# Smaller blocks in a triangular inverse, and another placing of the weight splits, in a two-layer hybrid trunk

## The chip, the cores and the metric

The kernel runs on one core of a Trainium2 chip. The metric is device time in microseconds (us) of one execution. The core's engines run side by side, each through a queue of its own in a fixed order: TensorE (PE, matrix products), VectorE (DVE), ScalarE (ACT), GpSimd (POOL) and SyncE (SP, here only an issuer of transfers).

## The reference

A causal decoder trunk of two layers for 256 tokens of width 1024, all in float32:

```
for each layer:
    x = LN(alpha * x + mixer(x))
    x = LN(alpha * x + relu(x @ W_in)**2 @ W_out)
layer 0 mixer: RWKV-7 time mixing (8 heads x 64) beside a block-sparse attention (4 heads x 128)
layer 1 mixer: dilated attention, three groups of 8 query heads x 128 over 8 shared k/v heads
RWKV-7, per head, for each token:
    S = S * w_t + (S @ a_t) b_t^T + v_t k_t^T ;  y_t = S @ r_t
```

The rest of the time mixing (token shift, decay, norms, gate, bonus) is done per token. With 256 tokens the sparse attention has one block and is plain causal attention.

## The kernel before, in words

**Weights.** All weights are 211 chunks of 128x1024 floats (512 KB), loaded in order by `Stream` into a ring of raw tiles (`load`, line 90, issued on SP). A chunk of number under `UNSPLIT` (17) is used as it is: a float32 product, which runs on PE in two passes. A later chunk is split (`split`): ACT casts the high part `hi` (line 95), DVE, or POOL for the twelve chunks listed in `ON_POOL`, subtracts to get the low part `lo` (line 97). A product with split operands is three passes, high by high, high by low and low by high (lines 225 and 230 to 232). The `hi`/`lo` tiles form a ring of places: `NW1` (4) in the first part, four more (`NW2`) from layer 0's MLP on. A split waits for a raw tile that has arrived and for a place that PE has left; the load of a raw tile waits for the split, or the product, that frees it.

**Order.** The Python order of the calls gives priorities; a scheduler then fixes one order for each engine when the kernel is built. `tc.high_priority()` and `early(...)` move work ahead. At run time an engine takes its queue strictly in order.

**First part (layer 0).** Chunks: 0 (`zwa`), 1 to 4 (k), 5 to 8 (v), 9 to 12 (`mv_chunk`, the attention's v), 13 to 16 (`r_proj`), 17 and 18 (`g_proj`), 19 to 26 (`m_proj`, the attention's q and k). `x_part` splits the input x into `xh` and `xl` for the three-pass products. RWKV-7 goes in two chunks of 128 tokens (c = 0, 1). For each the recurrence becomes a triangular system per head, whose unit triangular 128x128 matrix has to be inverted: `ab_mm` computes the strictly triangular part `abT[c]` and writes it to DRAM (`dA`); `g_load` (line 624) fetches the 64 diagonal blocks of 32x32 (16 matrices of four blocks), one per partition, into `gA`; `g_steps` inverts all of them on DVE by substitution, 31 steps of two instructions (lines 682, 684) of 31 to 256 elements; `g_back` writes the inverses to DRAM (`dT`, line 690) and reads them back as `Tall` (line 691) with a block's rows on partitions. `t_start` transposes them on DVE (line 746). Then PE doubles the block size: `w32`/`t32` go from 32 to 64 (line 757 multiplies `Tall` with `abT`), `w64`/`t64` from 64 to 128. `bk_step` transposes Bt and Kt (line 717), `mk_step` makes the masked products of a head (mask on DVE, line 655), `bonus` uses `bones` (line 644), and `gate_step` the gate.

The substitution step, j from 0 to 30:

```
n, m = 31 - j, j + 1
tmp[a, b] = gA[:, j, j + 1 + a] * gI[:, j, b]      # n x m, line 682
gI[:, j + 1:32, 0:m] += tmp                        # line 684
```

**Tails.** Every LayerNorm stands in a `tail`: DVE forms u and its statistics as the products of 128 tokens end (lines 260, 261), aggregates them (271, 272), POOL takes the power -0.5 of the variance (line 273), DVE scales (285, 286), PE transposes x (`trans`, line 297), ACT and DVE split it (`split_evac`, line 241). Token block 0 is normalized while PE multiplies for block 1. The MLP's first eight chunks follow (`by_token`; the squared relu is lines 414 to 416).

Of the kernel before, what the change touches and what calls it, by code (L numbers as in the profile page):

```python
# [36 lines left out]

NCHUNK = 211

UNSPLIT = 17  # L40
ON_POOL = (34, 36, 37, 38, 39, 42, 100, 150, 151, 161, 164, 169)


STATIONARY = [1] * 9 + [0] * 4 + [1] * 14 + [0] * 8
_MLP = [0] * 8 + [1] * 8 + [0] * 16 + ([1] * 8 + [0] * 8) * 2
STATIONARY += _MLP + [0] * 4 + [1] * 32 + [0] * 12 + _MLP
LINE, STAT_AT = 64, 56
NW1, NW2, NR, NR2 = 4, 4, 4, 2
NS4, NS2 = 13, 6
RIGHT = "right"  # L50
HS = 8 * (16 * P + 16)
NZ = 15
PC_MIX, PC_W0, PC_A0, PC_KK, PC_KA, PC_RK, PC_LG, PC_LB = 0, 15, 19, 23, 27, 31, 35, 39
NPAR = 43
# [72 lines left out]
def trunk(ctx: ExitStack, tc: tile.TileContext, w_all, x_nat, x_t, par_in, lora_in, gup2_in, ln_in,  # L127
# [35 lines left out]
    def tok_s(tok):  # L163
        return slice(tok * P, tok * P + P)
# [46 lines left out]
    def xraw(k):  # L211
        return xst[k // 2][:, k % 2]
# [237 lines left out]
    yl = [const.tile([P, 4, T], F32R, name=f"yl{i}") for i in range(2)]  # L450
    lora = pa.tile([P, 2, 512], F32, name="lora")
    nc.sync.dma_start(out=lora, in_=lora_in)
    bones = pa.tile([P, P], F32, name="bones")
    nc.sync.dma_start(out=bones, in_=bones_in)
    pmf = pa.tile([P, 4, P], F32, tag="s2", name="pmf", bufs=NS2)
    pmask = pa.tile([P, 4, P], U8, name="pmask")
    gup2 = pa.tile([P, 512], F32, name="gup2")
# [158 lines left out]
        dst = bass.AP(tensor=dA.tensor, offset=dA.offset + c * 8 * HS, ap=[[P, P], [HS, 8], [1, P]])  # L616
        nc.scalar.dma_start(out=dst, in_=abT[c])

    gA = pa.tile([64, 32, 32], F32, name="gA")
    gI = pa.tile([64, 32, 32], F32, name="gI")  # L620
    gtmp = pa.tile([64, 256], F32, name="gtmp")

    def g_load():
        nc.sync.dma_start(out=gA, in_=bass.AP(tensor=dA.tensor, offset=dA.offset, ap=[[32 * P + 32, 64], [P, 32], [1, 32]]))

    pend = pa.tile([P, 4, 1], F32, name="pend")

# [35 lines left out]
    def g_init():  # L663
        for c in range(2):
            nc.gpsimd.memset(X64s[c][0:32, :, 32:64], 0.0)
        nc.gpsimd.memset(gI, 0.0)
        nc.gpsimd.memset(gI.rearrange("p a b -> p (a b)")[:, 0:1024:33], 1.0)

    def ab_init(c):
        abT[c] = v8(s4(f"abT{c}"))  # L670
# [6 lines left out]

    def g_steps_(j0, j1):
        for j in range(j0, j1):
            n, m = 31 - j, j + 1  # L680
            tmp = gtmp[:, 0:n * m].rearrange("p (a b) -> p a b", a=n)
            nc.vector.tensor_tensor(tmp, gA[:, j, j + 1:32].unsqueeze(2).to_broadcast([64, n, m]),
                                    gI[:, j:j + 1, 0:m].to_broadcast([64, n, m]), MUL)
            nc.vector.tensor_tensor(gI[:, j + 1:32, 0:m], gI[:, j + 1:32, 0:m], tmp, ADD)


    Tall = pa.tile([P, 16, 32], F32, name="Tall")

    def g_back():
        nc.sync.dma_start(out=dT.rearrange("(p n) -> p n", p=64), in_=gI.rearrange("p a b -> p (a b)"))  # L690
        nc.sync.dma_start(out=Tall, in_=bass.AP(tensor=dT.tensor, offset=dT.offset, ap=[[32, P], [4096, 16], [1, 32]]))

    zg = {}
# [31 lines left out]
    def mv_chunk(ch):  # L725
        if ch == 0:
            accv.extend(bank(True) for t in range(2))
        hl = nxt()
        for kk in range(2):
            k = ch * 2 + kk  # L730
            for tok in range(2):
                nc.tensor.matmul(accv[tok], xraw(k)[:, tok_s(tok)], hl[:, half(kk)], start=k == 0, stop=k == KT - 1)

    def mv_end():
        vb = MV["vb"] = s4("vb").rearrange("p (c v) -> p c v", c=2)
# [4 lines left out]
    Tc, TTc, TT, Wc, X64 = {}, {}, {}, {}, {}  # L740
    odd = [(slice(b, b + 32), slice(b + 32, b + 64)) for b in (0, 64)]

    def t_start(c):
        Tc[c] = Tall[:, c * 8:c * 8 + 8, :]
        TTc[c] = pa.tile([P, 8, 32], F32, tag="TTc", name="TTc", bufs=2)
        nc.vector.transpose(TTc[c].rearrange("p h s -> p (h s)"), Tc[c].rearrange("p h s -> p (h s)"))
        TT[c] = v8(s4(f"TT{c}"))
        nc.gpsimd.memset(TT[c], 0.0)
        for b in range(0, P, 32):
            nc.scalar.copy(TT[c][b:b + 32, :, b:b + 32], TTc[c][b:b + 32])  # L750
# [251 lines left out]
    g_steps(12, 18)
    r_proj(0)
    r_proj(1)
    r_proj(2)
    mk_step(0, range(0, 4))
    g_steps(18, 24)
    bonus(0)
    g_steps(24, 31)
    r_proj(3)  # L1010
    g_back()
    s_init()
    t_start(0)
    g_proj(0)
# [280 lines left out]
def _constants():  # L1295
    f = np.float32
    half = 16
    inv = (f(500000.0) ** (-np.arange(half, dtype=f) / f(half))).astype(f)
    ang = np.arange(T, dtype=f)[None, :] * inv[:, None]
    cos, sin = np.cos(ang).astype(f), np.sin(ang).astype(f)  # L1300
    ropec = np.concatenate([cos, cos], axis=0)
    ropes = np.concatenate([-sin, sin], axis=0)
    ropec, ropes = [np.tile(t, (4, 1)) for t in (ropec, ropes)]
    t = np.arange(T)
    dist = t[:, None] - t[None, :]

    def add(ok):
        return np.where(ok, f(0), f(NEG)).astype(f)

    causal = add(dist >= 0)  # L1310
    cmask = np.concatenate([causal[:P, :P], causal[P:, :]], axis=1)
    gs = [add((dist >= 0) & (dist <= 128)), add((dist >= 0) & (dist % 4 == 0)), add((dist >= 0) & (dist % 16 == 0))]
    dmask = np.concatenate([g[:P, :P] for g in gs] + [g[P:, :] for g in gs], axis=1)
    s = np.arange(P)
    strict = (s[:, None] < s[None, :])
    incl = (s[:, None] <= s[None, :])
    pmask = np.stack([incl, strict, incl, strict], axis=1).astype(f)
    bones = (s[:, None] // 64 == s[None, :] // 64).astype(f)
# [22 lines left out]
```

## Time and profile before

| | |
|---|---|
| median of three runs | 721.17 us (720.55 to 723.44) |
| the profiled execution | 720.38 us |
| its span in the trace | 718.6 us |
| PE busy | 97% of the span |
| DVE, ACT, POOL busy | 65%, 48%, 10% |
| weight splits on DVE, on POOL | 182 and 12 |
| mean granted TensorE clock | 0.992 of full speed |

The profile is of one execution. Busy time counts an engine as working while an instruction runs; a row of a timeline gives start, duration, the instruction with its tiles, and in brackets the idle time of that engine ahead of it with what ended the wait.

### The profile page before, as it was taken

What the parts mean: (1) busy time and instruction counts of PE and PEld (TensorE: products, weight loads), DVE (VectorE), ACT (ScalarE), POOL (GpSimd) and SP (SyncE); (2) the same over time, 40 slices, a digit from 0 to 9 for tenths busy, and PEclk for the clock granted to TensorE, in tenths of its full rate; (3) what the DMA queues carried; (4) which work ended last, traced back from release to release, by engine and by line L of the source; (5) the groups of instructions that cost most, each with busy time, mean ns of one, the idle gap of its engine ahead of it and who ended that gap; (6) DMA issues with size and microseconds to landing.
All of it is one profiled execution on the core that took longest, in us unless ns stands there. A gap on an engine that the chain in (4) does not pass through costs nothing. (4 is left out here: it accounts for less than half of the span.)

```text
span 718.6 us, 11530 instructions
## 1 busy us (share of the span) xinstructions
PE 696.8 (97%) x4572; PEld 621.0 (86%) x4572; DVE 463.7 (65%) x753; ACT 344.4 (48%) x515; POOL 70.9 (10%) x75
## 2 busy tenths in 40 slices
PE   9999999997999999999999999999999999999995
PEld 7867898986889889989879999998878888998985
DVE  3747985659686445546597767775488654464645
ACT  4712357253375335445164666656337543454520
POOL 3000000026100000000020121111131110000002
PEclk9999999998999999999999999999999999999998
DMA  8366362156584666565078543444357465655401
GB/s 322 123 185 192 132 189 77 60 179 237 171 292 148 205 201 192 192 193 191 29 263 304 165 152 126 166 151 157 106 160 258 162 201 186 204 182 187 133 1 59
DMA packets 40759, 122.74 MB, mean 171 GB/s; under 512 B 8129, under 2 KB 11073, under 8 KB 40577
## 3 DMA queue, kind: packets, MB, share of 16 engines
q1 hardware_dynamic: 38048, 120.07, 50.9%
q10 hardware_dynamic: 2656, 1.93, 0.9%
q8 instruction: 36, 0.59, 0.3%
q14 instruction: 19, 0.15, 0.1%
HBM read 119.63 MB, written 2.36 MB: 170 GB/s over the span
## 5 line engine op out<-in xcount | busy, mean ns | idle before, releaser
L97 DVE TENSOR_TENSOR lo<-raw,hi 128x1024 fp32r<-128x1024 f32 x182 | 231.9, 1278 | 150.7 <-ACT hi L95 145.9
L95 ACT CAST hi<-raw 128x1024 fp32r<-128x1024 f32 x194 | 202.3, 1050 | 201.3 <-PE bank L231 97.8
L225 PE MATMUL bank<-xh,hi 128*128 128x256 f32 x720 | 175.3, 284 | 2.1 <-DVE rm L870 2.1
L225 PE MATMUL bank<-xl,hi 128*128 128x256 f32 x720 | 173.2, 280 | 0.0
L225 PEld LDWEIGHTS bank<-xh,hi 128*128 128x128 f32 x720 | 135.2, 188 | 3.9 <-DVE rm L870 2.5
L225 PEld LDWEIGHTS bank<-xl,hi 128*128 128x128 f32 x720 | 135.4, 188 | 0.6
L231 PE MATMUL bank<-hi,hl 128*128 128x512 f32 (+1 forms) x288 | 105.8, 368 | 1.9 <-DVE hl L241 1.9
L232 PE MATMUL bank<-lo,hh 128*128 128x512 f32 (+1 forms) x288 | 105.3, 366 | 0.0
L230 PE MATMUL bank<-hi,hh 128*128 128x512 f32 (+1 forms) x288 | 104.6, 367 | 0.3 <-ACT hh L240 0.3
L225 PE MATMUL bank<-xh,lo 128*128 128x256 f32 x720 | 100.3, 280 | 0.0
L225 PEld LDWEIGHTS bank<-xh,lo 128*128 128x128 f32 x720 | 90.9, 188 | 0.2
L231 PEld LDWEIGHTS bank<-hi,hl 128*128 128x128 f32 x288 | 54.3, 189 | 11.1 <-DVE hl L241 2.5
L230 PEld LDWEIGHTS bank<-hi,hh 128*128 128x128 f32 x288 | 54.2, 189 | 9.5 <-ACT hh L240 0.5
L232 PEld LDWEIGHTS bank<-lo,hh 128*128 128x128 f32 x288 | 54.3, 188 | 8.8
L217 PE MATMUL bank<-xst,raw 128*128 128x256 f32 x208 | 47.0, 386 | 0.3 <-DMA xst<-in_x_t_dram 0.3
L217 PEld LDWEIGHTS bank<-xst,raw 128*128 128x128 f32 x208 | 40.1, 194 | 7.4 <-DMA xst<-in_x_t_dram 1.2
L273 POOL TENSOR_TENSOR rs<-rs,mhalf 128x1 f32<-128x1 f32 x8 | 7.7, 962 | 321.3 <-DVE rs L272 321.3
L232 PE MATMUL bank<-lo,xh 128*128 128x512 f32 x96 | 37.7, 393 | 0.6 <-DVE lo L97 0.5
L230 PE MATMUL bank<-hi,xh 128*128 128x512 f32 x96 | 38.0, 396 | 0.0
L231 PE MATMUL bank<-hi,xl 128*128 128x512 f32 x96 | 37.5, 391 | 0.1
L97 POOL TENSOR_TENSOR lo<-raw,hi 128x1024 fp32r<-128x1024 f32 x12 | 30.3, 2533 | 56.2 <-ACT hi L95 50.5
L260 DVE SCALAR_TENSOR_TENSOR u<-x,bank 128x512 f32<-128x512 f32 (+1 forms) x17 | 11.0, 651 | 24.4 <-PE bank L232 24.4
(237 smaller groups left out, 838.4 us busy)
## 6 DMA issues: line engine op xcount, KB each, us to landing
raw<-in_w_all_dram SPq DMA_DIRECT2D x210, 512.0 KB, 4.1
g<-in_ln_dram SPq DMA_DIRECT2D x4, 512.0 KB, 5.4
b<-in_ln_dram SPq DMA_DIRECT2D x4, 512.0 KB, 6.7
dA<-abT ACTq DMA_DIRECT2D x2, 512.0 KB, 3.6
x<-in_x_nat_dram SPq DMA_DIRECT2D x1, 1024.0 KB, 4.8
dmask<-in_dmask_dram SPq DMA_DIRECT2D x1, 576.0 KB, 6.6
xst<-in_x_t_dram ACTq DMA_DIRECT2D x2, 256.0 KB, 5.5
xst<-in_x_t_dram SPq DMA_DIRECT2D x2, 256.0 KB, 5.7
```

Of the source, the lines that this page charges most:

```text
L95: self.nc.scalar.copy(hi[:, cols], r[:, cols])
L97: eng.tensor_tensor(lo[:, cols], r[:, cols], hi[:, cols].bitcast(F32), ALU.subtract)
L217: nc.tensor.matmul(ps, hl[:, k * P:(k + 1) * P], xraw(k), start=k == 0, stop=k == KT - 1)
L225: nc.tensor.matmul(ps, w[:, k * P:(k + 1) * P], a[:, k, :], start=n == 0, stop=n == 3 * KT - 1)
L230: nc.tensor.matmul(acc, ah, hi[:, cols], start=first, stop=False)
L231: nc.tensor.matmul(acc, al, hi[:, cols], start=False, stop=False)
L232: nc.tensor.matmul(acc, ah, lo[:, cols], start=False, stop=last)
L260: nc.vector.scalar_tensor_tensor(self.u[:, c], self.x[:, self.tok, c], ALPHA, ps, MUL, ADD)
L273: nc.gpsimd.tensor_tensor(rs, rs, mhalf, ALU.pow)
```

## The change

Blocks of 16x16 in place of 32x32: 128 blocks on 128 partitions, 15 steps of two instructions with at most 64 elements. `g_back` multiplies the inverses by two parity columns, so that each block lands in its half of a 32-wide row (`gP`). `t_start` gets a doubling from 16 to 32 on PE: for each token chunk 32 products of 32x32 (new line 763), a mask multiply on DVE (765), 32 more products (769), an add (771) and two transposes in all. `bones` carries the mask and the parity columns in 34 more columns. `UNSPLIT` falls from 17 to 11, so that chunks 11 to 16 are split; `x_part` therefore moves ahead of `mv_chunk(1)`. `ON_POOL` is empty: every low part is made on DVE. `NW2` is 6, which gives ten places in the second part in place of eight. All substitution steps and `g_back` now stand ahead of `r_proj`.

```diff
@@ -37,18 +37,19 @@
 
 NCHUNK = 211
 
-UNSPLIT = 17
-ON_POOL = (34, 36, 37, 38, 39, 42, 100, 150, 151, 161, 164, 169)
+UNSPLIT = 11
+ON_POOL = ()
 
 
 STATIONARY = [1] * 9 + [0] * 4 + [1] * 14 + [0] * 8
 _MLP = [0] * 8 + [1] * 8 + [0] * 16 + ([1] * 8 + [0] * 8) * 2
 STATIONARY += _MLP + [0] * 4 + [1] * 32 + [0] * 12 + _MLP
 LINE, STAT_AT = 64, 56
-NW1, NW2, NR, NR2 = 4, 4, 4, 2
+NW1, NW2, NR, NR2 = 4, 6, 4, 2
 NS4, NS2 = 13, 6
 RIGHT = "right"
-HS = 8 * (16 * P + 16)
+GB = 16
+HS = (P // GB) * (GB * P + GB)
 NZ = 15
 PC_MIX, PC_W0, PC_A0, PC_KK, PC_KA, PC_RK, PC_LG, PC_LB = 0, 15, 19, 23, 27, 31, 35, 39
 NPAR = 43
@@ -450,8 +451,10 @@
     yl = [const.tile([P, 4, T], F32R, name=f"yl{i}") for i in range(2)]
     lora = pa.tile([P, 2, 512], F32, name="lora")
     nc.sync.dma_start(out=lora, in_=lora_in)
-    bones = pa.tile([P, P], F32, name="bones")
-    nc.sync.dma_start(out=bones, in_=bones_in)
+    bonesx = pa.tile([P, P + 34], F32, name="bones")
+    nc.sync.dma_start(out=bonesx, in_=bones_in)
+
+    bones, mlow, par2 = bonesx[:, 0:P], bonesx[:, P:P + 32], bonesx[:, P + 32:P + 34]
     pmf = pa.tile([P, 4, P], F32, tag="s2", name="pmf", bufs=NS2)
     pmask = pa.tile([P, 4, P], U8, name="pmask")
     gup2 = pa.tile([P, 512], F32, name="gup2")
@@ -616,12 +619,14 @@
         dst = bass.AP(tensor=dA.tensor, offset=dA.offset + c * 8 * HS, ap=[[P, P], [HS, 8], [1, P]])
         nc.scalar.dma_start(out=dst, in_=abT[c])
 
-    gA = pa.tile([64, 32, 32], F32, name="gA")
-    gI = pa.tile([64, 32, 32], F32, name="gI")
-    gtmp = pa.tile([64, 256], F32, name="gtmp")
+
+    gA = pa.tile([P, GB, GB], F32, name="gA")
+    gI = pa.tile([P, GB, GB], F32, name="gI")
+    gP = pa.tile([P, GB, 2, GB], F32, name="gP")
+    gtmp = pa.tile([P, GB * GB // 4], F32, name="gtmp")
 
     def g_load():
-        nc.sync.dma_start(out=gA, in_=bass.AP(tensor=dA.tensor, offset=dA.offset, ap=[[32 * P + 32, 64], [P, 32], [1, 32]]))
+        nc.sync.dma_start(out=gA, in_=bass.AP(tensor=dA.tensor, offset=dA.offset, ap=[[GB * P + GB, P], [P, GB], [1, GB]]))
 
     pend = pa.tile([P, 4, 1], F32, name="pend")
 
@@ -664,7 +669,7 @@
         for c in range(2):
             nc.gpsimd.memset(X64s[c][0:32, :, 32:64], 0.0)
         nc.gpsimd.memset(gI, 0.0)
-        nc.gpsimd.memset(gI.rearrange("p a b -> p (a b)")[:, 0:1024:33], 1.0)
+        nc.gpsimd.memset(gI.rearrange("p a b -> p (a b)")[:, 0:GB * GB:GB + 1], 1.0)
 
     def ab_init(c):
         abT[c] = v8(s4(f"abT{c}"))
@@ -677,17 +682,19 @@
 
     def g_steps_(j0, j1):
         for j in range(j0, j1):
-            n, m = 31 - j, j + 1
+            n, m = GB - 1 - j, j + 1
             tmp = gtmp[:, 0:n * m].rearrange("p (a b) -> p a b", a=n)
-            nc.vector.tensor_tensor(tmp, gA[:, j, j + 1:32].unsqueeze(2).to_broadcast([64, n, m]),
-                                    gI[:, j:j + 1, 0:m].to_broadcast([64, n, m]), MUL)
-            nc.vector.tensor_tensor(gI[:, j + 1:32, 0:m], gI[:, j + 1:32, 0:m], tmp, ADD)
+            nc.vector.tensor_tensor(tmp, gA[:, j, j + 1:GB].unsqueeze(2).to_broadcast([P, n, m]),
+                                    gI[:, j:j + 1, 0:m].to_broadcast([P, n, m]), MUL)
+            nc.vector.tensor_tensor(gI[:, j + 1:GB, 0:m], gI[:, j + 1:GB, 0:m], tmp, ADD)
 
 
     Tall = pa.tile([P, 16, 32], F32, name="Tall")
 
     def g_back():
-        nc.sync.dma_start(out=dT.rearrange("(p n) -> p n", p=64), in_=gI.rearrange("p a b -> p (a b)"))
+        for i in range(2):
+            nc.vector.tensor_scalar_mul(gP[:, :, i, :], gI, par2[:, i:i + 1])
+        nc.sync.dma_start(out=dT.rearrange("(p n) -> p n", p=P), in_=gP.rearrange("p a i b -> p (a i b)"))
         nc.sync.dma_start(out=Tall, in_=bass.AP(tensor=dT.tensor, offset=dT.offset, ap=[[32, P], [4096, 16], [1, 32]]))
 
     zg = {}
@@ -729,7 +736,10 @@
         for kk in range(2):
             k = ch * 2 + kk
             for tok in range(2):
-                nc.tensor.matmul(accv[tok], xraw(k)[:, tok_s(tok)], hl[:, half(kk)], start=k == 0, stop=k == KT - 1)
+                if not isinstance(hl, tuple):
+                    nc.tensor.matmul(accv[tok], xraw(k)[:, tok_s(tok)], hl[:, half(kk)], start=k == 0, stop=k == KT - 1)
+                    continue
+                xstat(accv[tok], xh[:, k, tok_s(tok)], xl[:, k, tok_s(tok)], hl, half(kk), k == 0, k == KT - 1)
 
     def mv_end():
         vb = MV["vb"] = s4("vb").rearrange("p (c v) -> p c v", c=2)
@@ -740,10 +750,27 @@
     Tc, TTc, TT, Wc, X64 = {}, {}, {}, {}, {}
     odd = [(slice(b, b + 32), slice(b + 32, b + 64)) for b in (0, 64)]
 
+    blocks = [slice(b, b + 32) for b in range(0, P, 32)]
+
     def t_start(c):
-        Tc[c] = Tall[:, c * 8:c * 8 + 8, :]
+
+        D = Tall[:, c * 8:c * 8 + 8, :]
+        DT = pa.tile([P, 8, 32], F32, tag="DT", name="DT", bufs=2)
+        nc.vector.transpose(DT.rearrange("p h s -> p (h s)"), D.rearrange("p h s -> p (h s)"))
+        psW = bank()[:, 0:T].rearrange("p (h s) -> p h s", h=8)
+        for h in range(8):
+            for r in blocks:
+                nc.tensor.matmul(psW[r, h, :], abT[c][r, h, r], D[r, h, :], start=True, stop=True)
+        W = pa.tile([P, 8, 32], F32, tag="W16", name="W16", bufs=2)
+        nc.vector.tensor_tensor(W, psW, mlow.unsqueeze(1).to_broadcast([P, 8, 32]), MUL)
+        psT = bank()[:, 0:T].rearrange("p (h s) -> p h s", h=8)
+        for h in range(8):
+            for r in blocks:
+                nc.tensor.matmul(psT[r, h, :], W[r, h, :], DT[r, h, :], start=True, stop=True)
         TTc[c] = pa.tile([P, 8, 32], F32, tag="TTc", name="TTc", bufs=2)
-        nc.vector.transpose(TTc[c].rearrange("p h s -> p (h s)"), Tc[c].rearrange("p h s -> p (h s)"))
+        nc.vector.tensor_tensor(TTc[c], psT, DT, ADD)
+        Tc[c] = pa.tile([P, 8, 32], F32, tag="Tc", name="Tc", bufs=2)
+        nc.vector.transpose(Tc[c].rearrange("p h s -> p (h s)"), TTc[c].rearrange("p h s -> p (h s)"))
         TT[c] = v8(s4(f"TT{c}"))
         nc.gpsimd.memset(TT[c], 0.0)
         for b in range(0, P, 32):
@@ -990,25 +1017,22 @@
     ab_mm(0)
     v_tok(1)
     ab_mm(1)
-    mv_chunk(1)
-    mv_chunk(2)
-    g_load()
     for q in range(4):
         x_part(q)
+    mv_chunk(1)
+    g_load()
+    mv_chunk(2)
     mv_chunk(3)
     mv_end()
-    g_steps(0, 12)
+    g_steps(0, GB - 1)
+    g_back()
     pend_step()
-    g_steps(12, 18)
     r_proj(0)
     r_proj(1)
     r_proj(2)
     mk_step(0, range(0, 4))
-    g_steps(18, 24)
     bonus(0)
-    g_steps(24, 31)
     r_proj(3)
-    g_back()
     s_init()
     t_start(0)
     g_proj(0)
@@ -1315,7 +1339,9 @@
     strict = (s[:, None] < s[None, :])
     incl = (s[:, None] <= s[None, :])
     pmask = np.stack([incl, strict, incl, strict], axis=1).astype(f)
-    bones = (s[:, None] // 64 == s[None, :] // 64).astype(f)
+    b32 = np.arange(32)
+    low = (s[:, None] % 32 >= 16) & (b32[None, :] < 16)
+    bones = np.concatenate([s[:, None] // 64 == s[None, :] // 64, low, s[:, None] % 2 == np.arange(2)[None, :]], axis=1).astype(f)
     return {"ropec": ropec, "ropes": ropes, "cmask": cmask, "dmask": dmask, "pmask": pmask, "bones": bones}
```

PE around the first product on `Tall` (line 757 before, 763 in the change; line 225, or 226, is a three-pass product of the projections, `hi_71` a place of a chunk, `qk` the attention's scores). Before:

```order
L225 MATMUL bank_82<-xl,hi_71 128x256
L225 MATMUL bank_82<-xh,lo_72 128x256 x5
L757 MATMUL bank_75<-Tall,abT_376 32x32 x16
L757 MATMUL bank_77<-Tall,abT_378 32x32 x16
L225 MATMUL bank_82<-xh,lo_72 128x256 x3
```

In the change:

```order
L713 MATMUL bank_82<-zg,gup_130 128x256
L824 MATMUL bank_75<-vN,mkt 128x64 x5
L226 MATMUL bank_77<-xh,hi_71 128x256
L226 MATMUL bank_77<-xl,hi_71 128x256
L226 MATMUL bank_77<-xh,hi_71 128x256
L226 MATMUL bank_77<-xl,hi_71 128x256
L763 MATMUL bank_78<-Tall,abT_377 32x32 x32
L763 MATMUL bank_80<-Tall,abT_379 32x32 x19
L769 MATMUL bank_79<-DT,W_700 32x32 x32
```

Before, the products on `Tall` stand inside the second half of the `m_proj` chunks, behind the first attention scores; in the change they stand behind seven heads' products with v and four products of an `m_proj` chunk.

SP's queue around `g_back` (`raw` tiles are weight loads). Before:

```order
L90 DMA raw1_64<-in_w_all_dram 128x1024
L90 DMA raw2_65<-in_w_all_dram 128x1024
L690 DMA dT_163<-gI_165 64x1024
L90 DMA raw3_66<-in_w_all_dram 128x1024
L90 DMA raw0_63<-in_w_all_dram 128x1024
L691 DMA Tall_170<-dT_163 128x16x32
```

In the change:

```order
L91 DMA raw0_63<-in_w_all_dram 128x1024
L91 DMA raw1_64<-in_w_all_dram 128x1024
L697 DMA dT_163<-gP_166 128x512
L91 DMA raw2_65<-in_w_all_dram 128x1024
L698 DMA Tall_171<-dT_163 128x16x32
L91 DMA raw3_66<-in_w_all_dram 128x1024
```

Before, two weight loads stand between the write of `dT` and the read of `Tall`; in the change it is one.

DVE in the first tail, from the first u (line 260, or 261) to the first x (line 286, or 287). Before:

```order
L260 SCALAR_TENSOR_TENSOR u_1413<-x_1402,bank4_79 128x512
L260 SCALAR_TENSOR_TENSOR u_1413<-x_1402,bank7_82 128x512
L261 BN_STATS st_1414<-u_1413 128x6 x2
L271 BN_AGGR mv_1466<-st_1414 128x2
L272 TENSOR_SCALAR rs_1467<-mv_1466 128x1
L285 SCALAR_TENSOR_TENSOR u_1413<-u_1413,mv_1466,g0_1405 128x512 x2
L260 SCALAR_TENSOR_TENSOR u_1415<-x_1402,bank0_75 128x512
L286 SCALAR_TENSOR_TENSOR x_1402<-u_1413,rs_1467,b1_1407 128x512
```

In the change:

```order
L98 TENSOR_TENSOR lo8_1601<-raw4_1604,hi8_1600 128x1024
L261 SCALAR_TENSOR_TENSOR u_1620<-x_1609,bank7_82 128x512
L261 SCALAR_TENSOR_TENSOR u_1620<-x_1609,bank5_80 128x512
L262 BN_STATS st_1621<-u_1620 128x6 x2
L98 TENSOR_TENSOR lo9_1603<-raw5_1605,hi9_1602 128x1024
L272 BN_AGGR mv_1673<-st_1621 128x2
L261 SCALAR_TENSOR_TENSOR u_1622<-x_1609,bank1_76 128x512
L273 TENSOR_SCALAR rs_1674<-mv_1673 128x1
L286 SCALAR_TENSOR_TENSOR u_1620<-u_1620,mv_1673,g0_1612 128x512
L262 BN_STATS st_1623<-u_1622 128x6
L287 SCALAR_TENSOR_TENSOR x_1609<-u_1620,rs_1674,b1_1614 128x512
```

In the change two low parts (`lo8`, `lo9`) stand ahead of x in this queue, and the second token block's first u and its statistics too.

## Rows read from the trace of the kernel before

**Rows 1.** The page: busy us by engine; memory traffic; the chain that ended last, by engine.

```profile
PE 696.8 (97%) x4572; PEld 621.0 (86%) x4572; DVE 463.7 (65%) x753; ACT 344.4 (48%) x515; POOL 70.9 (10%) x75
...
HBM read 119.63 MB, written 2.36 MB: 170 GB/s over the span
...
PE 41%; DVE 4%; issue 2%; DMA 1%; POOL 0%; ACT 0%; POOLq 0%; SPq 0%; DVEq 0%; ACTq 0%
```

**Rows 2.** Timeline of PE, 55 to 110 us: start, us, instruction, count [idle before <-releaser].

```profile
58.54 10.52 PE L217 MATMUL bank<-xst,raw 128*128 128x256 f32 x48
...
77.83 0.28 PE L225 MATMUL bank<-xh,hi 128*128 128x256 f32 x1
...
80.64 0.59 PE L644 MATMUL bank<-km,bones 128*128 128x256 f32 x2
82.18 0.66 PE L717 MATMUL bank<-ident,Bt 128*128 128x128 f32 x4 [0.95 <-DVE zg L491]
...
87.69 0.66 PE L717 MATMUL bank<-ident,Kt 128*128 128x128 f32 x4 [0.50 <-DVE mkt L655]
...
92.33 0.48 PE L225 MATMUL bank<-xh,hi 128*128 128x256 f32 x2
...
106.17 1.20 PE L757 MATMUL bank<-Tall,abT 32*32 32x32 f32 x64
```

**Rows 3.** Timeline of DVE, 57 to 98 us, the substitution.

```profile
57.50 0.18 DVE L682 TENSOR_TENSOR gtmp<-gA,gI 64x31 f32<-64x31 f32 x1 [7.86 <-DMA gA<-dA]
...
57.96 0.21 DVE L682 TENSOR_TENSOR gtmp<-gA,gI 64x60 f32<-64x60 f32 x1
...
95.06 1.21 DVE L97 TENSOR_TENSOR lo<-raw,hi 128x1024 fp32r<-128x1024 f32 x1
...
96.33 0.47 DVE L710 SCALAR_TENSOR_TENSOR zv<-zv,par,gate 128x256 f32<-128x256 f32 x1
96.72 0.18 DVE L682 TENSOR_TENSOR gtmp<-gA,gI 64x31 f32<-64x31 f32 x1
96.83 0.47 DVE L710 SCALAR_TENSOR_TENSOR zv<-zv,par,gate 128x256 f32<-128x256 f32 x1
```

**Rows 4.** The page, costliest groups: busy us, mean ns of one, idle before.

```profile
L95 ACT CAST hi<-raw 128x1024 fp32r<-128x1024 f32 x194 | 202.3, 1050 | 201.3 <-PE bank L231 97.8
```

**Rows 5.** Timelines of SP and of DVE, 97 to 108 us.

```profile
97.48 0.49 SPq L690 DMA_DIRECT2D dT<-gI  x1
...
106.06 0.77 DVE L746 STREAM_TRANSPOSE TTc<-Tall 128x256 f32<-128x256 f32 x2 [0.48 <-DMA Tall<-dT]
```

**Rows 6.** Timelines of POOL, DVE and PE around the first tail, 167 to 186 us.

```profile
167.07 4.77 POOL L97 TENSOR_TENSOR lo<-raw,hi 128x1024 fp32r<-128x1024 f32 x2 [5.72 <-PE bank L232]
171.79 1.00 POOL L273 TENSOR_TENSOR rs<-rs,mhalf 128x1 f32<-128x1 f32 x1
...
169.43 0.15 DVE L272 TENSOR_SCALAR rs<-mv 128x1 f32<-128x1 f32 x1
...
173.57 2.23 DVE L286 SCALAR_TENSOR_TENSOR x<-u,rs,b 128x512 f32<-128x512 f32 x1
...
185.88 1.40 DVE L286 SCALAR_TENSOR_TENSOR x<-u,rs,b 128x512 f32<-128x512 f32 x2
...
175.86 1.11 PE L297 MATMUL bank<-ident,x 128*128 128x128 f32 x4 [3.58 <-DVE x L286]
```

**Rows 7.** Windows: us, PE, PEld, DVE, ACT, POOL busy (instructions), clock, DMA share, GB/s.

```profile
174.69:181.52 6.83, 5.27 (x16) 4.07 (x17) 5.65 (x6) 3.26 (x5) 3.35 (x2) 0.50 0.53 161
```

**Rows 8.** Timelines of DVE and of PE at the third tail.

```profile
523.29 2.49 DVE L286 SCALAR_TENSOR_TENSOR x<-u,rs,b 128x512 f32<-128x512 f32 x1
...
525.83 0.66 PE L297 MATMUL bank<-ident,x 128*128 128x128 f32 x4 [1.65 <-DVE x L286]
```

**Rows 9.** Timelines of DVE and of PE in the MLP of layer 1.

```profile
556.86 2.48 DVE L416 TENSOR_TENSOR s<-r 128x512 f32<-128x512 f32 x1 [0.83 <-ACT r L414]
...
560.52 0.50 PE L231 MATMUL bank<-hi,hl 128*128 128x512 f32 x1 [1.52 <-DVE hl L241]
```

## The prediction, as recorded before the result

> **What bounds the kernel now.** I read the engines' busy shares and the chain of waits first. TensorE (PE) works 97% of the span and carries 41% of the chain, VectorE (DVE) 4%, the transfers 1% [rows 1]. So a part of the change is worth what it takes from PE's own work, plus the gaps in PE's row that it closes, less those that it opens. Next came PE's timeline, for the price of a product and for the gaps; then the timelines of DVE, SyncE's queue (SP) and GpSimd (POOL) at each gap, for what ended last. The profiled execution took 720.38 us; the median of the three runs is 721.17, 0.8 higher. I sum against 720.38. About 0.5% (3.6 us) is what a measurement of this kernel can tell from no change, so "faster" begins below 717.6 and "slower" above 724.8.
>
> **Part one: chunks, inverse, order (up to about 110 us).** Everything here runs on PE in one fixed order.
>
> *Chunks 11 to 16 split.* An unsplit chunk costs PE a third of 10.52 us, 3.5 (the row at 58.54: 48 passes, three chunks) [rows 2]. A split one costs 80.64 - 77.83 = 2.8 [rows 2]. Six chunks: **-4.0**.
>
> *Doubling from 16 to 32.* 128 more products of 32x32, in two passes each. 64 such passes took 1.20 us, 19 ns each (the row at 106.17) [rows 2], so 256 take **+4.8**. By the columns alone (a 256-column pass of chunk 17 comes every 2.81/24 = 0.117 us, so 32 columns every 15 ns) it would be 3.7, the low end. The Trainium skill, "TensorE: Matmul & The Clock Gate", section "Wait — 56ns, not 53.3ns?", has matmuls never start closer than about 25 ns however few their columns; as an estimate by that page the 256 passes would take 6.4 and the whole 1.6 more. The row's 19 ns disagrees with the page, and the row decides.
>
> *Gaps that go.* PE waits 0.95 us at 82.18 and 0.50 at 87.69, both for DVE [rows 2], while DVE works off the 62 steps of the substitution. With 30 short steps these waits lose their cause: **-1.45**, ends 0 and -1.45.
>
> *The new wait, for Tall.* In the new order PE meets the first product on Tall (line 763) after chunks 11 to 18 and only four products of chunk 21 (the PE rows of the change). When does PE come there? Chunk 17 began at 77.83 and at 92.33 the same work was done and 3.5 us more: 20 passes of chunk 19 (20 x 0.117 = 2.3), the transposes of Kt (0.6) and the last head (0.6, estimated as the two products at 80.64) [rows 2]. So PE needs 92.33 - 3.5 - 77.83 - 1.45 = 9.5 us from chunk 17's start, which now is 77.83 - 4.0 = 73.9, and comes to Tall at 83.4.
>
> When does Tall come? gA was there at 57.50 [rows 3]; the chunks newly split put work ahead of its transfer, half a split: 58.1. Then DVE has 30 steps. Alone, two take 0.46 (57.50 to 57.96), 0.23 each; slipped between other work, one costs 0.11 (96.72 to 96.83) [rows 3]. I take 0.15: 4.5. Between them stand seven splits at 1.21 (8.5), twelve instructions of the r projections at 0.39 (96.33 to 96.72: 4.7), five of the mk and zv kind at 0.5 (2.5) [rows 3] and the two that make gP (0.6): 20.8 in all, so 78.9. A second path says the same: just ahead of gP stands the split of chunk 21, which needs the places that PE frees with chunk 17. Sixteen passes after 73.9, at 75.8, ScalarE (ACT) can cast, 1.05 [rows 4], then 1.21 and 0.6: 78.7. The trip over memory took from 97.48 to 106.06, 8.6 us [rows 5]. Tall is there at 87.5, PE at 83.4: a wait of **+4.1**. Ends: one load of 512 KB less stands ahead of Tall on SP (3.1 us of the trip at the span's 170 GB/s [rows 1]), which gives 1.0; with steps at 0.23 the queue is 2.4 longer, which gives 6.5. Queued behind the waiting product on PE are chunks 19 and 20; their places come free later, and ACT, DVE and then SP's loads wait for these. I add nothing for that: transfers hold 1% of the chain before [rows 1], so the stream can catch up. The two later waits in the new doubling (the mask multiply, then the add) have 19 products of the other half ahead of them, and I cost them at nothing; without that cover each would cost about the 0.47 of a 256-element instruction (the row at 96.33) [rows 3].
>
> *Clock after that wait.* In the one long wait of the first tail PE stood idle from 172.28 (175.86 - 3.58), and from 174.69 the granted clock was 0.50, the 1.2 GHz level, for 6.83 us with 5.27 of PE work in it [rows 6, 7]. After a wait of only 1.65 four transposes took 0.66 against 1.11 after the 3.58 [rows 6, 8]: no fall there. A wait of 4.1 should see the fall 2.4 us in; of 6.83 us then 1.7 are idle and 5.1 work. Of these I count the 2.7 that are not 32x32 passes, whose 19 ns are not set by columns, at half: **+1.4**, ends 0 and 2.6.
>
> Part one: -4.0 + 4.8 - 1.45 + 4.1 + 1.4 = **+4.85**.
>
> **Part two: weight splits off POOL, more places.** *First tail.* DVE had made its variance by 169.6, but the power on POOL started at 171.79, after two splits of 4.77 us on that engine: some 2.2 late. Then one instruction of line 286 took 2.23 beside POOL's next splits, where two took 1.40 at 185.88, 0.70 each: 1.5 more [rows 6]. Without POOL's splits x comes 3.7 earlier; but two splits now stand on DVE ahead of it (the DVE rows of the change), 2 x 1.21 = 2.4. Net 1.3 to 1.4, so the 3.58 gap becomes 2.2. That is shorter than the 2.4 after which the clock fell, so the lost half of 5.27 comes back too, 2.6: **-4.0**, ends 0 and -6.2.
>
> *Third tail.* The same instruction took 2.49 at 523.29 and PE waited 1.65 behind it [rows 8]; at 0.70 the gap closes: **-1.65**, ends 0 and -1.65. *MLP of layer 1.* Line 416, an instruction of the same size, took 2.48 while POOL made a split, and PE waited 1.52 for what follows it [rows 9]. It gains 1.8, and one split of 1.21 more stands in the queue, whose idle 0.83 takes part of it: between 0.6 and 1.5, I take **-1.1**. The two extra pairs of places I cost at nothing: the gaps of PE that I found there end on DVE's own instructions, none on a place that comes free; what covers a wait for a place is PE's work, 97% of the span [rows 1], and without that cover a late split would show as a gap of its 1.21.
>
> Sum: 4.85 - 4.0 - 1.65 - 1.1 = -1.9. **720.4 - 1.9 = 718.5.**
>
> **Rivals.**
> *Tall in time.* If the trip takes 4.5 instead of 8.6, the wait and the clock's fall go: 718.5 - 5.5 = **713.0**. For it: part of the 8.6 is spent behind loads. Against: the two paths to gP agree, and neither leaves PE work for the trip.
> *First tail gains nothing.* The two splits on DVE, with their casts, eat all that POOL's absence gives: 718.5 + 4.0 = **722.5**. The Trainium skill, "Perfetto Trace Analysis", section "Optimizing Scalar/DVE Operations", lets work go from a saturated DVE even to GpSimd, and adds that this might not help since both share a port; the rows bear out the caution, 2.23 against 0.70 beside POOL.
> *DVE becomes the bound of the tails: slower.* Six of POOL's splits belonged to the first tail. If all six stand ahead of x, it comes 6 x 1.21 - 3.7 = 3.6 later than before: a gap of 7.2 where I have 2.2, the clock's 2.6 unrecovered, and 1.65 lost in the third tail the same way: 718.5 + 5.0 + 2.6 + 1.65 = **727.8**. It turns slower at 724.8: with the clock lost, when some three splits more than the two of the order stand ahead. Against: the order shows two.
> The change does what it says; I find no rival there.
>
> **How the numbers follow.** Forecast 0.48, Tall in time 0.16, first tail without gain 0.20, DVE the bound 0.16. The forecast's own range goes from 718.5 - 3.1 - 1.4 = 714.0 to 718.5 + 2.4 + 1.2 = 722.1. The range for 8 in 10 takes all of that, the upper part of "Tall in time" and most of "no gain" with its bounds: 712.0 to 724.0. Faster: half of the forecast (0.24), all of Tall in time (0.16), 0.02 of no gain: 0.42. Same: 0.23 + 0.13 = 0.36. Slower: 0.01 + 0.05 + 0.16 = 0.22.
>
> **What would show it.** Right: chunks 11 to 16 at 2.8 us each; the 64 32x32 products of one half in about 2.4; a wait of some 4 us ended by Tall's transfer ahead of line 763, near 83 us, and a granted clock of 0.5 behind it; no power waiting on POOL; a gap of about 2.2 ahead of the first tail's transposes at full clock; lines 286 and 416 at 0.7. Wrong: no wait at Tall, splits waiting for places, a gap over 3.6 in the first tail, or DVE's splits ending PE's waits elsewhere.

## The result, and the profile after

The changed kernel takes 716.50 us (median of 14 runs, 713.69 to 720.30) against 721.48 for the kernel before on the same chips: a ratio of 0.9925, 95% interval 0.9901 to 0.9949. It is faster by some 5 us; 718.5 was forecast, with a range of 712.0 to 724.0. The profiled execution took 715.71 us, its span is 713.6 us.

From the page of the changed kernel: the engines' busy time, the chain by engine (the instructions and waits that lead to the last instruction), and one group (busy us, mean ns of one, idle before).

```profile
PE 695.4 (97%) x4868; PEld 624.7 (88%) x4868; DVE 456.7 (64%) x747; ACT 349.8 (49%) x521; POOL 39.3 (6%) x63
...
PE 45%; DVE 0%; issue 0%; ACT 0%; POOLq 0%; POOL 0%; DVEq 0%
...
L98 DVE TENSOR_TENSOR lo<-raw,hi 128x1024 fp32r<-128x1024 f32 x200 | 247.8, 1245 | 156.6 <-ACT hi L96 154.6
```

PE's busy time is nearly that of before [rows 1], its idle time has gone from 21.8 to 18.2 us of the span, and DVE from 4% of the chain to nothing: most of the gain is in waits, not in work. All 200 splits are on DVE, so nothing stands in front of POOL's power.

Part one, PE's timeline (start, us, instruction, count, idle before and its releaser):

```profile
65.48 0.50 PE L657 MATMUL bank<-AR,Bt 64*128 64x128 f32 x4
...
67.28 0.50 PE L657 MATMUL bank<-AR,Bt 64*128 64x128 f32 x4 [0.87 <-DVE AR L639]
...
80.79 0.66 PE L724 MATMUL bank<-ident,Bt 128*128 128x128 f32 x4 [1.39 <-DVE zv L651]
...
86.18 1.18 PE L763 MATMUL bank<-Tall,abT 32*32 32x32 f32 x102
87.51 0.47 PE L769 MATMUL bank<-DT,W 32*32 32x32 f32 x33
89.35 0.45 PE L769 MATMUL bank<-DT,W 32*32 32x32 f32 x31 [1.38 <-issue]
...
97.52 0.75 PE L769 MATMUL bank<-DT,W 32*32 32x32 f32 x64
...
104.14 1.20 PE L784 MATMUL bank<-Tc,abT 32*32 32x32 f32 x64
```

A raw chunk cost 3.5, a split one 2.8 [rows 2]: the heads' products (line 657) begin at 65.48 where before they began at 68.99, 3.5 earlier after five of the six chunks. The rest is given back. PE waits 0.87 and 1.39 us for DVE at the masked products and the transposes; it meets Tall without a wait, though only just (DVE had Tall at 85.98, PE's first product on it starts at 86.18); inside line 769 stands a gap of 1.38 us that ends on nothing the profile shows ("issue"). The extra 32x32 products are cheap: 64 passes of line 769 take 0.75 us, while 64 of line 784, the old step from 32 to 64, still take the 1.20 of [rows 2].

The inverse's way out, DVE's and SP's timelines:

```profile
78.00 0.61 DVE L696 TENSOR_SCALAR gP<-gI,bones 128x256 f32<-128x256 f32 x2
...
85.98 0.77 DVE L759 STREAM_TRANSPOSE DT<-Tall 128x256 f32<-128x256 f32 x2 [0.17 <-DMA Tall<-dT]
...
78.64 0.33 SPq L697 DMA_DIRECT2D dT<-gP  x1
```

gP ends and its write is issued at 78.64 (forecast: 78.9); DVE has Tall at 85.98 (forecast: 87.5), after a trip of 7.3 us.

The granted clock, from the windows (us, then busy us of PE, PEld, DVE, ACT and POOL, then clock, DMA share, GB/s):

```profile
90.50:93.91 3.41, 3.41 (x16) 3.30 (x16) 0.80 (x2) 2.30 (x6) 0.00 (x0) 0.50 0.02 5
107.56:110.98 3.42, 3.42 (x41) 3.36 (x35) 2.54 (x6) 0.00 (x0) 0.00 (x0) 0.50 0.26 95
```

Two stretches of 3.4 us at 0.50, the 1.2 GHz level: the first behind a row of 32x32 products (lines 763 and 769) and the gap of 1.38 us in it, the second behind others (lines 784 and 796), with PE idle for only 0.12 of the 3.56 us before it. PE was busy through both, so at half speed they cost at most 1.7 us each, an estimate.

The first tail, timelines of POOL, DVE and PE:

```profile
175.61 0.90 POOL L274 TENSOR_TENSOR rs<-rs,mhalf 128x1 f32<-128x1 f32 x1 [13.12 <-DVE rs L273]
...
175.29 0.15 DVE L273 TENSOR_SCALAR rs<-mv 128x1 f32<-128x1 f32 x1
...
176.62 0.74 DVE L287 SCALAR_TENSOR_TENSOR x<-u,rs,b 128x512 f32<-128x512 f32 x1
...
178.69 0.75 DVE L287 SCALAR_TENSOR_TENSOR x<-u,rs,b 128x512 f32<-128x512 f32 x1
...
177.89 0.60 PE L298 MATMUL bank<-ident,x 128*128 128x128 f32 x4
179.16 0.73 PE L231 MATMUL bank<-hi,xh 128*128 128x512 f32 x2 [0.67 <-ACT xh L241]
```

Variance at 175.29, power right behind it at 175.61, line 287 at 0.74 in place of 2.23 [rows 6]. The transposes of x follow at 177.89 without a wait; only 0.67 us (and 0.36 a little later) are lost at the products that use x, in place of 3.58 and a fall of the clock [rows 6, 7].

Third tail and the MLP of layer 1, DVE and PE:

```profile
521.67 0.73 DVE L287 SCALAR_TENSOR_TENSOR x<-u,rs,b 128x512 f32<-128x512 f32 x1
...
522.47 0.66 PE L298 MATMUL bank<-ident,x 128*128 128x128 f32 x4
...
553.70 0.68 DVE L417 TENSOR_TENSOR s<-r 128x512 f32<-128x512 f32 x1
...
555.57 0.50 PE L232 MATMUL bank<-hi,hl 128*128 128x512 f32 x1 [0.38 <-DVE hl L242]
```

Line 287 and line 417 take 0.73 and 0.68 [rows 8, 9]; PE's 1.65 is gone and its 1.52 is 0.38.

Put in stages: DVE's first u of the first tail starts at 171.10, against 166.68 before, so part one is 4.4 us *longer* (at 48 us the two profiles still stand level: the first part's second row of `mv_chunk` products starts at 48.14 before and at 47.98 in the change). The second LayerNorm's power starts at 351.81 against 352.83, 1.0 ahead, so the first tail gave back 5.4. The third's, at 518.65 against 520.26, is 1.6 ahead, and at the end the span is 5.0 shorter.

### The profile page after: what moved, and what is told of

The parts are those of the page before. It is cut to its first block, busy times and chain, and to the rows that moved or that the text cites. A ratio compares the mean times of both kernels' runs of the same rounds, so it can differ in the third digit from the quotient of the medians.

```text
span 713.6 us, 12129 instructions
## 1 busy us (share of the span) xinstructions
PE 695.4 (97%) x4868; PEld 624.7 (88%) x4868; DVE 456.7 (64%) x747; ACT 349.8 (49%) x521; POOL 39.3 (6%) x63
## 5 line engine op out<-in xcount | busy, mean ns | idle before, releaser
L98 DVE TENSOR_TENSOR lo<-raw,hi 128x1024 fp32r<-128x1024 f32 x200 | 247.8, 1245 | 156.6 <-ACT hi L96 154.6
L96 ACT CAST hi<-raw 128x1024 fp32r<-128x1024 f32 x200 | 208.2, 1050 | 215.7 <-PE bank L232 99.7
L226 PE MATMUL bank<-xh,hi 128*128 128x256 f32 x752 | 185.5, 286 | 1.6 <-DVE rm L897 1.0
L226 PE MATMUL bank<-xl,hi 128*128 128x256 f32 x752 | 183.1, 282 | 0.0
L226 PEld LDWEIGHTS bank<-xh,hi 128*128 128x128 f32 x752 | 142.7, 190 | 3.7 <-DVE rm L897 1.2
L226 PEld LDWEIGHTS bank<-xl,hi 128*128 128x128 f32 x752 | 143.1, 190 | 0.5
L226 PEld LDWEIGHTS bank<-xh,lo 128*128 128x128 f32 x752 | 94.8, 188 | 0.0
L218 PE MATMUL bank<-xst,raw 128*128 128x256 f32 x144 | 32.1, 381 | 0.9 <-DMA xst<-in_x_t_dram 0.9
L218 PEld LDWEIGHTS bank<-xst,raw 128*128 128x128 f32 x144 | 27.0, 190 | 6.1 <-DMA xst<-in_x_t_dram 2.2
L231 PE MATMUL bank<-hi,yh 128*128 128x512 f32 x64 | 25.7, 401 | 0.0
```

The source lines that it names most:

```text
L96: self.nc.scalar.copy(hi[:, cols], r[:, cols])
L98: eng.tensor_tensor(lo[:, cols], r[:, cols], hi[:, cols].bitcast(F32), ALU.subtract)
L218: nc.tensor.matmul(ps, hl[:, k * P:(k + 1) * P], xraw(k), start=k == 0, stop=k == KT - 1)
L226: nc.tensor.matmul(ps, w[:, k * P:(k + 1) * P], a[:, k, :], start=n == 0, stop=n == 3 * KT - 1)
L231: nc.tensor.matmul(acc, ah, hi[:, cols], start=first, stop=False)
```

## The experiments

Theory: the gain comes from taking the splits off POOL, part one costs time. Rivals: the gain comes from the extra places, or from the split chunks.

**Before, POOL's splits to DVE alone.**

```diff
-ON_POOL = (34, 36, 37, 38, 39, 42, 100, 150, 151, 161, 164, 169)
+ON_POOL = ()
```

> The kernel before with ON_POOL empty and nothing else. Theory (the gain of the change lies in the two tails and the MLP of layer 1, and comes from taking the splits off POOL): the waits of 3.58 and 1.65 us ahead of the transposes of the first and third tail and the 1.52 in the MLP of layer 1 shrink to under 1 us together each, the granted clock does not fall in the first tail, and the time falls by 8 to 10 us, below the changed kernel: about 711. Rival (DVE cannot take the splits; the gain came from the other parts): 719 to 721, the waits stay where they were.

Measured: 712.04 us, ratio 0.9868 (0.9845 to 0.9891). This one line is worth more than the whole change, whose interval does not reach it. PE at the first and the third tail:

```profile
175.46 0.60 PE L297 MATMUL bank<-ident,x 128*128 128x128 f32 x4
177.14 0.74 PE L230 MATMUL bank<-hi,xh 128*128 128x512 f32 x2 [1.08 <-ACT xh L240]
...
519.23 0.66 PE L297 MATMUL bank<-ident,x 128*128 128x128 f32 x4
```

No wait at the transposes in either, 1.08 us behind the first, and the mean granted clock is 0.997.

**The change with POOL's splits back.** The diff the other way round, in the changed kernel.

> The changed kernel with the old ON_POOL list. Theory: the waits on POOL's power and on line 287 return, the time rises by 7 to 10 us to about 724, slower than before, because part one alone costs some 4 us. Rival: within 2 us of the changed kernel.

Measured: 723.55, ratio 1.0021 (0.9999 to 1.0043): the change without that line is no gain. POOL, DVE and PE in the first tail:

```profile
170.29 7.52 POOL L98 TENSOR_TENSOR lo<-raw,hi 128x1024 fp32r<-128x1024 f32 x3 [5.78 <-ACT hi L96]
177.77 0.99 POOL L274 TENSOR_TENSOR rs<-rs,mhalf 128x1 f32<-128x1 f32 x1
...
178.88 2.74 DVE L287 SCALAR_TENSOR_TENSOR x<-u,rs,b 128x512 f32<-128x512 f32 x1
...
181.67 1.12 PE L298 MATMUL bank<-ident,x 128*128 128x128 f32 x4 [6.19 <-DVE x L287]
```

Three splits of 7.52 us stand ahead of the power, line 287 takes 2.74 beside the next, and PE waits 6.19.

**First tail and later splits apart.** The kernel before with half of the list each:

```diff
-ON_POOL = (34, 36, 37, 38, 39, 42, 100, 150, 151, 161, 164, 169)
+ON_POOL = (100, 150, 151, 161, 164, 169)
```

> The kernel before with chunks 34 to 42 off POOL, and the six later ones (100 to 169) still on it. Theory (most of the gain is the first tail's wait and the fall of the clock behind it, 3.58 + 2.6 us): 6 us less than before, 715 to 716, and the 1.65 and 1.52 us waits at the third tail and in the MLP of layer 1 stay. Rival (my term of 4.0 was right because two splits on DVE take the rest): 717.

Measured: 716.52, ratio 0.9918 (0.9891 to 0.9944). PE at the first and the third tail:

```profile
175.77 0.73 PE L230 MATMUL bank<-hi,xh 128*128 128x512 f32 x2 [1.07 <-ACT xh L240]
...
520.72 0.66 PE L297 MATMUL bank<-ident,x 128*128 128x128 f32 x4 [1.66 <-DVE x L286]
```

```diff
-ON_POOL = (34, 36, 37, 38, 39, 42, 100, 150, 151, 161, 164, 169)
+ON_POOL = (34, 36, 37, 38, 39, 42)
```

> The kernel before with chunks 100 to 169 off POOL, and 34 to 42 still on it. Theory: the waits of 1.65 and 1.52 us shrink and the first tail's 3.58 stays: 2.5 to 3.5 us less than before, 718. Rival (these waits have another cause): 721.

Measured: 717.23, ratio 0.9927 (0.9900 to 0.9955), a little more than expected. PE at the same places:

```profile
176.74 0.66 PE L297 MATMUL bank<-ident,x 128*128 128x128 f32 x4 [3.52 <-DVE x L286]
...
525.98 0.66 PE L297 MATMUL bank<-ident,x 128*128 128x128 f32 x4
```

Each half removes its own wait and leaves the other's. 5.3 and 4.6 us (against 721.79) make 9.8 together, about the 9.1 (against 721.16) of the whole line.

**Eight places in place of ten.** The changed kernel with

```diff
-NW1, NW2, NR, NR2 = 4, 6, 4, 2
+NW1, NW2, NR, NR2 = 4, 4, 4, 2
```

> The changed kernel with NW2 = 4, eight places in place of ten. Theory (the extra places are worth nothing, because no gap of PE ended on a place): within 1 us of the changed kernel, 716 to 717. Rival (the gain after the first tail comes from the places): 3 us or more above it, with waits of PE on line 98 or 96 in the MLPs.

Measured: 715.88, ratio 0.9926 (0.9903 to 0.9949), the change's own. The extra places are worth nothing that shows.

**Chunks 11 to 16 unsplit again, new inverse kept.**

```diff
-UNSPLIT = 11
+UNSPLIT = 17
```

> The changed kernel with chunks 11 to 16 unsplit again. Theory (PE bounds part one, a split chunk saves 0.7 us of PE): 4.0 us of PE work more, and less for DVE and ACT, so that the two waits of 0.87 and 1.39 us for DVE at 66 and 79 us shrink: 718 to 720.5. Rival (DVE bounds part one): within 1 us of the changed kernel, or faster.

Measured: 714.20, ratio 0.9899 (0.9874 to 0.9924). My theory missed: with 4 us more of PE work the kernel is not slower. Part one on PE:

```profile
74.91 0.75 PE L763 MATMUL bank<-Tall,abT 32*32 32x32 f32 x64
...
77.65 0.74 PE L769 MATMUL bank<-DT,W 32*32 32x32 f32 x64 [1.20 <-DVE W L765]
...
86.25 0.66 PE L724 MATMUL bank<-ident,Bt 128*128 128x128 f32 x4 [0.65 <-DVE zv L651]
```

Tall is there at 74.91, since DVE and ACT have six splits less; the 64s of short products stand apart, the unexplained gap and both falls of the clock are absent, and the waits of 0.87 and 1.39 are 0.65 in all at those places (1.20 stands at line 769).

**The change without the new inverse.** Before's blocks of 32x32 and 31 steps, and these steps and `g_back` where the kernel before has them, between the r chunks; the rest as changed.

```diff
-UNSPLIT = 17
-ON_POOL = (34, 36, 37, 38, 39, 42, 100, 150, 151, 161, 164, 169)
+UNSPLIT = 11
+ON_POOL = ()
...
-NW1, NW2, NR, NR2 = 4, 4, 4, 2
+NW1, NW2, NR, NR2 = 4, 6, 4, 2
...
-    mv_chunk(1)
-    mv_chunk(2)
-    g_load()
     for q in range(4):
         x_part(q)
+    mv_chunk(1)
+    g_load()
+    mv_chunk(2)
```

> The change without its new inverse: blocks of 32x32 and 31 steps as before, but UNSPLIT = 11, the new order of the splits of x, ON_POOL empty, NW2 = 6. Theory (PE bounds part one, so the shorter substitution saves nothing and the 128 extra products cost): the kernel before without POOL's splits (712.0) less 4.0 us for six split chunks, 708. Rival (with six splits more, DVE cannot also hold the long substitution): PE waits for DVE around 60 to 100 us, 711 or more.

Measured: 732.67, ratio 1.0166 (1.0141 to 1.0192). The rival holds, by far more than it said. The last step on DVE, SP's write, PE at Tall, and the window behind:

```profile
110.04 0.18 DVE L684 TENSOR_TENSOR gI<-gI,gtmp 64x31 f32<-64x31 f32 x1
...
110.58 0.49 SPq L690 DMA_DIRECT2D dT<-gI  x1
...
119.19 1.92 PE L760 MATMUL bank<-Tall,abT 32*32 32x32 f32 x64 [8.87 <-DMA Tall<-dT]
...
113.69:147.82 34.13, 25.48 (x243) 23.57 (x244) 6.30 (x19) 12.14 (x29) 0.00 (x0) 0.50 0.07 15
```

The six splits and the products' other work fill DVE's queue between the steps: the last one ends at 110.22, dT is issued at 110.58 where it was 97.48 [rows 5], and PE, ahead of it now, waits 8.87. Then 34.13 us run at half clock with 25.48 us of work, some 13 us lost by an estimate of half the work. With chunks 11 and 12 unsplit it is the same in small:

```diff
-UNSPLIT = 17
-ON_POOL = (34, 36, 37, 38, 39, 42, 100, 150, 151, 161, 164, 169)
+UNSPLIT = 13
+ON_POOL = ()
```

(in the kernel before)

> The kernel before with ON_POOL empty and UNSPLIT = 13, old inverse. Theory: 712.0 less 4 x 0.7 = 709.2. Rival (the long substitution leaves DVE no time for four splits more): 711.5 or more, PE waiting for lo tiles near 80 to 100 us.

Measured: 727.37, ratio 1.0073 (1.0044 to 1.0101). PE at Tall:

```profile
117.38 1.92 PE L757 MATMUL bank<-Tall,abT 32*32 32x32 f32 x64 [3.22 <-DMA Tall<-dT]
```

So the new inverse, with its steps placed earlier, is what makes the split chunks bearable: among kernels without POOL's splits, the old inverse takes 712.0 with chunks 11 to 16 raw and 732.7 with them split; the new one 714.2 and 715.9 to 716.5. Whether the 31 steps of the old inverse, placed as early, would do it too was not tried, so the shorter steps and the earlier place are not told apart.

**Short products apart.** The changed kernel with `t_start(1)` behind `m_proj(0, 2)`.

```diff
     mk_step(0, range(4, 8))
     m_proj(0, 0)
-    t_start(1)
     early(bk_step, Bt)
...
     m_proj(0, 2)
+    t_start(1)
     early(bk_step, Kt)
```

> The changed kernel with the second half's start of the doubling moved two chunks later, so that the first 64 32x32 products and the next 64 no longer stand in one row on PE. Theory (the unexplained gap of 1.38 us inside line 769 and the fall of the clock behind it come from 102 and then 32 short products in a row): both go, 3 us less than the changed kernel, 713. Rival (gap and fall belong to the late arrival of Tall): the same as the changed kernel, 716.

Measured: 714.15, ratio 0.9906 (0.9882 to 0.9930); the intervals overlap, so the profile has to speak. PE:

```profile
67.59 0.50 PE L657 MATMUL bank<-AR,Bt 64*128 64x128 f32 x4 [1.26 <-DVE AR L639]
...
79.36 0.66 PE L724 MATMUL bank<-ident,Bt 128*128 128x128 f32 x4 [1.72 <-DVE zg L494]
...
87.38 0.75 PE L763 MATMUL bank<-Tall,abT 32*32 32x32 f32 x64
...
88.84 0.75 PE L769 MATMUL bank<-DT,W 32*32 32x32 f32 x64
90.68 0.49 PE L657 MATMUL bank<-AR,Bt 64*128 64x128 f32 x2 [1.08 <-issue]
...
103.32 1.20 PE L784 MATMUL bank<-Tc,abT 32*32 32x32 f32 x64
```

No fall of the clock between 65 and 112 us, as expected, but the gap of unknown cause is still there, 1.08 us, now behind line 769. So the gap does not come from the long row. The clock is less clear. Three other runs speak against the row as the cause of the fall. With POOL's splits back, the same row (102 and 64 passes, from 88.20) was followed by full clock until 106.6, and the first fall came ahead of it, at 82.7, behind a wait of 1.31. In the two reordered kernels below the short products stand apart as here, and the clock fell at 92.9 in both. And the kernel before without its later POOL splits has the part one of the kernel before, yet its profile shows a fall from 109.3 to 112.7 that three profiles of the same part one (before, list empty, first tail off) do not. What makes the clock fall in part one stays open. The waits of 1.26 and 1.72 remain.

**Half the chunks.** The changed kernel with UNSPLIT = 13.

> The changed kernel with UNSPLIT = 13: the attention's v chunks 11 and 12 unsplit, the four r chunks split. Theory: PE's price of a chunk holds, 0.7 us for each of four chunks split against the kernel with UNSPLIT = 17 (714.2), and the products on Tall stay apart: 711.5. Rival (DVE's waits eat the gain): 714 or more.

Measured: 717.38, ratio 0.9940 (0.9903 to 0.9976). PE at Tall, and the window behind:

```profile
82.41 0.74 PE L763 MATMUL bank<-Tall,abT 32*32 32x32 f32 x64 [2.04 <-DMA Tall<-dT]
...
83.20:90.03 6.83, 6.83 (x85) 4.89 (x86) 4.10 (x9) 1.76 (x5) 0.00 (x0) 0.50 0.39 136
```

The rival: PE waits 2.04 for Tall, then 6.83 us run at 0.50.

**Reordered to dodge the waits.** From the kernel with the short products apart:

```diff
     r_proj(2)
+    r_proj(3)
     mk_step(0, range(0, 4))
     bonus(0)
-    r_proj(3)
...
+    m_proj(0, 0)
     bonus(1)
     mk_step(0, range(4, 8))
-    m_proj(0, 0)
-    early(bk_step, Bt)
     m_proj(0, 1)
+    bk_step(Bt)
...
-    early(bk_step, Kt)
+    bk_step(Kt)
```

> The kernel of the run e7_after_spread (714.15) with the masked products of the first four heads behind all four r chunks, the other four heads and the bonus one chunk later, and the transposes of Bt and Kt no longer moved ahead. Theory (the 4.2 us that six split chunks save PE are eaten by waits on DVE at these products and transposes, 1.26 and 1.72 us and smaller ones, because PE meets them too early): these waits fall below 1 us together, 711. Rival (DVE's queue is full there, a wait only moves): 714 or more.

Measured: 717.70, ratio 0.9926 (0.9901 to 0.9950). PE, and a window:

```profile
72.78 0.39 PE L226 MATMUL bank<-xh,hi 128*128 128x256 f32 x1 [1.67 <-DVE zr L494]
...
86.96 0.74 PE L763 MATMUL bank<-Tall,abT 32*32 32x32 f32 x64 [2.22 <-DMA Tall<-dT]
...
90.36 0.38 PE L657 MATMUL bank<-AR,Bt 64*128 64x128 f32 x2 [0.96 <-issue]
...
92.87:96.28 3.41, 3.41 (x13) 2.94 (x12) 1.32 (x2) 1.73 (x4) 0.00 (x0) 0.50 0.24 42
```

The rival: the waits at the old places are gone, but 1.67 us stand at the next product that needs DVE and 2.22 at Tall, and the clock falls again.

> As e10_reordered, but the transposes of Bt and Kt still moved ahead. Theory: the transposes wait for a bank that DVE has to empty, so 0.5 to 1.5 us of wait stay at them: 711.5 to 713. Rival: no difference from e10_reordered.

That run gave 715.24, ratio 0.9919 (0.9897 to 0.9941): not to be told from the other, with waits of 1.80, 1.11 and 0.71 (the last for Tall). In these kernels, with the chunks split, DVE sets the pace of part one, and order only moves the wait.

## Why the prediction was right, and which terms failed

The sign, the range and the place of gain and loss held: part one longer, both tails and the MLP shorter. The sum was 3 us short of the gain. By the prediction's own bound of 717.6 its 718.5 was still no change that could be told, and "faster", which came, had 0.42.

*Split chunks, -4.0.* Right: 3.5 after five chunks. *Doubling, +4.8.* Mis-sized: 1.18, 0.43, 0.47, 0.45 and 0.75 for its five pieces, 3.3 us. The row it was priced by, line 757, takes its operands from two groups of 32 partitions in turn; the new products go through all four, and 64 passes take 0.75. That this is the reason was not tried by itself.

*Gaps that go, -1.45.* Wrong in kind. I removed the waits because DVE's steps are shorter and did not ask where PE, 0.7 earlier with every chunk, next meets DVE: 0.87 and 1.39 took their place. *Wait for Tall, +4.1.* DVE's queue was right to 0.3 us and the trip 1.3 too long, but PE came at 86 rather than 83.4, held up by those two waits, and the wait at Tall was nil. That was luck, by 0.2 us; the wait is real all the same: 0.71, 2.04 and 2.22 in three variants, 3.22 and 8.87 with the long inverse. The prediction's second path to gP agreed only by a slip: the row at 77.83 is the start of chunk 18, and chunk 17 began at 74.84. PE's arrival does not depend on the name, but the places of chunk 17 come free 3 us earlier than the path has it. In the change ACT's cast for chunk 21 starts at 74.03 and the split on DVE at 76.86, behind the last step, so DVE's queue alone set the time of gP. With the 1.38 of unknown cause and smaller ones, gaps of 3.9 us stand on PE in part one against 2.5 before: 1.4 more, where the two terms made 2.65. *Clock, +1.4.* Wrong cause in this run: no long wait, yet two falls, at most 3.4 us by the estimate above, whose cause is open. Summed, -4.2 (the sixth chunk counted), +3.3, +1.4 and +3.4 make 3.9 of the measured 4.4; 4.85 was forecast. Nearly right by errors that cancel.

*First tail, -4.0.* Mis-sized: 5.4 by stages, 5.3 as a run of its own. The mechanism was right (power behind POOL's splits, line 286 slowed beside them, the clock). But I charged both splits of DVE to the gap, and only one stands between the first u and x: x is whole 6.3 us after that u (171.10 to 177.36), where it took 9.1 (166.68 to 175.80), 2.9 less and not 1.3. And I did not ask how many products of the other token block now stand in front of the transposes: PE comes to them 6.8 us after the first u (177.89), where it was 5.6 (172.28). Together that is more than the 3.58, and no wait was left there. *Third tail, -1.65*: right. *MLP, -1.1*: 1.14. The rest, some 1.2 us, lies half between the second and the third LayerNorm and half behind the third; the later splits cost more than the two waits that I priced (4.6 as a run of their own, for 2.75).

*Rivals.* Tall in time did happen, because PE was late and not because the trip was short. That DVE would eat the first tail's gain, or become the bound of the tails, is refuted by the run with POOL's list emptied, where DVE makes all the splits of the tails too.

What stays open: what makes the clock fall in part one, and the gap of 0.96 to 1.38 us without a releaser, seen in five kernels some two us after the first product on Tall, and absent in the three others with the new inverse (POOL's splits back, chunks 11 to 16 raw, chunks 11 and 12 raw). Whether PE's instructions arrive late there was not tried. The two are also why part one's sum, 3.9 of 4.4, is an account and not a proof.

The fastest of all these kernels has the smallest edit: the kernel before with POOL's list empty, 712.04 us.

## What to carry to other kernels

Help from an engine that shares work with the critical one is priced by what stands behind it in its own queue and beside it on the other engine, not by its free time: POOL was 10% busy, and its twelve splits cost 9 us. Before shortening work on the bounding engine, find where it then meets the next one; two parts of a change that each look like a gain can both be losses. Against the 712.0 of the emptied list alone, the split chunks without the new inverse took 732.7 and both together 716.5; the new inverse without the split chunks, at 714.2, is no gain that shows. Take one line of a change by itself before building on all of it.

## What the runs showed of the hardware

The granted clock fell to 0.50 behind 32x32 products although PE had been busy: 0.12 us idle in the 3.56 us before the fall at 107.56. Such falls come and go from run to run. Over the 14 runs of the changed kernel the run with mean clock 0.997 took 714.0 us, three with 0.990 took 718.9 to 720.3. All four runs of the fastest kernel have 0.997, and they lie between 711.58 and 712.24.

Beside a split on POOL, DVE instructions of 512 elements that read two tiles in SBUF (lines 286 and 416) took 2.2 to 2.7 us, and 0.7 without one. Lines 260 (one tile in SBUF, one PSUM bank) and 261 (one tile in SBUF) took 0.67 and 0.68 beside the same split, at 172.97 and 175.73 us of the kernel before.

64 passes of 32x32 took 0.75 us over four groups of 32 partitions, 12 ns apiece, and 1.20 over two, 19 ns, in the same kernel. The Trainium skill, "TensorE: Matmul & The Clock Gate", section "Wait — 56ns, not 53.3ns?", has matmuls never start closer than about 25 ns. Both rows lie below that, and the measurement decides.
